# Attention of one encoder layer: TensorE in an order written by hand, long rows beside short ones, output products two steps behind

## The chip, the cores and the metric

The kernel runs on one core of a Trainium2 chip. The metric is device time in microseconds (us) of one execution, the median of several. The engines are TensorE (PE; its weight loads are listed as PEld), VectorE (DVE), ScalarE (ACT), GpSimd (POOL) and SyncE (SP), which issues most DMAs. Each takes its own instructions in order and waits on semaphores for the others.

## The reference, cut to what matters

One layer on a sequence of 2048 positions of width 1024: a norm, one projection to queries, keys and values, two kinds of attention side by side, an output projection, and a gated feed-forward network with a short convolution.

```python
h = rmsnorm(x, attn_norm_g)
qa, ka, va, qb, kb, vb = split(h @ w_in, 6)          # 6 x 512 columns
# A: 8 heads of 64; a query sees 8 chunks of 64 to its left and its own chunk
pa = softmax(qa ka^T / 8 + rel_bias, over the band);  oa = pa @ va
# B: 4 heads of two maps of 64; a query sees all chunks up to its own
p1, p2 = softmax(q1 k1^T / 8 + t5_bias), softmax(q2 k2^T / 8 + t5_bias)
ob = rmsnorm((p1 - lam * p2) @ vb) * subln_g * 0.8
x = x + concat(oa, ob) @ w_out
u = causal_dwconv(rmsnorm(x) @ w_up);  gate, val = split(u)
out = rmsnorm(x + (silu(gate) * val) @ w_down)
```

## The kernel before, in words

Every float32 operand is held as two float16 parts (high and low), and a product is three matmuls (high x high, high x low, low x high).

**Stages.** First the norm of x is transposed into `hT`, four tiles of 512 positions (`make_h`). Then comes attention, in eight passes that are called heads here: `ORDER` is 4, 5, 0, 6, 1, 7, 2, 3, where 4 to 7 are the B heads and 0 to 3 are pairs of A heads. Then comes the output projection (`out_proj`, in two halves of four units), and from there the feed-forward network, which the change does not touch.

**A head** has 16 rows of 128 queries. A row i of a B head reaches over (i+1) x 128 keys; a row of an A head reaches over at most 640. For a row (`attn_a` L452, `attn_b` L503):

1. TensorE computes scores in pieces of up to 512 keys, for two maps, into a bank of PSUM each (`scores`, L426 and L428; four banks in all). The low part of the queries has 64 rows of weights, the high part 128.
2. VectorE adds the bias and takes the running maximum (L474 in A, L524 in B: one instruction for a piece and a map), then the negative scaled maximum (`nb`, L478, L527).
3. ScalarE takes the exponentials with their sums (L481, L530). In B, VectorE forms sums, reciprocal and `ratio` (L533, L536, L538) and subtracts the second map from the first (L546; for some groups ScalarE and GpSimd do it, L543 and L544).
4. ScalarE copies to float16 (`phl`, high part, L482, L548), and the low part is a subtraction: on VectorE for one map of an A row and on GpSimd for the other (L483), on GpSimd in B (L549).
5. SyncE's DMA transposes `phl` into `pt` (in groups of at most 1024 keys), TensorE multiplies `pt` by the values (L495, L557: the output products), and VectorE scales the result into `osb` (L497, L559).

Of the tiles between these steps there are two `phl`, three `pt`, and eight of `St`, the rows of scores.

**Projections.** Beside the rows of a head, TensorE projects the rest of this head's queries and the next head's keys and values, 24 matmuls of 512 columns for 512 positions (`project`, L372). The next head's weights are loaded, scaled and split at the head's start; a small matmul sums their squares over the partitions (L146).

**What sets the order.** A scheduler places each engine's instructions by priority: the order of the program's text, with 1000 places of advantage for the attention rows (`attend`, `HA`) and for the splits of a projection (`HP`). It also weighs when it thinks operands will be ready, so on each engine the rows, the projections and the output products of several rows are mixed.

Of the kernel before, what the change touches and what calls it, by code (L numbers as in the profile page):

```python
# [18 lines left out]
P = 128  # L19
# [13 lines left out]
HA = 1000  # L33
KF = True
# [31 lines left out]
def kernel(  # L66
# [135 lines left out]
    with ExitStack() as at:  # L202
# [116 lines left out]
        def load_w(w, p, j, first=False, raw=None):  # L319
# [3 lines left out]
                             .rearrange("p (c n) -> p c n", c=NC))  # L323
            E, RE, gs = scale_of(all_rows(ss, bank_a), ga, 2.0 ** 13, 2.0 ** -80)
# [40 lines left out]
        def project(w, tg, j):  # L365

            hl, h = w["hl"][j], hT[tg]
            ps = ps_mm.tile([P, TG], F32, name="mm")
            n = 0
            for c in range(NC):  # L370
                for a, b in TERMS:
                    nc.tensor.matmul(ps, lhsT=hl[:, a, c, :], rhs=h[:, b, c, :], start=n == 0, stop=n == 3 * NC - 1)  # L372
                    n += 1
            return ps

        def proj_k(w, tg):

            ks = kv.tile([P, 2, TG], F16, name="ks")
            ps = project(w, tg, 1)
# [3 lines left out]
            return ks  # L383

        def proj_v(w, tg):


            vs = kv.tile([P, 2, 4, P], F16, name="vs")
            if "first" in w:
                hl, h = w["hl"][2], hT[tg]  # L390
                ps = ps_mm.tile([P, 4, P], F32, name="mm")
                for t in range(4):
                    n = 0
                    for c in range(NC):
                        for a, b in TERMS:
                            nc.tensor.matmul(ps[:, t], lhsT=h[:, a, c, t * P:(t + 1) * P], rhs=hl[:, b, c, :],
                                             start=n == 0, stop=n == 3 * NC - 1)
                            n += 1
                with tc.high_priority(offset=HP):
                    split(vs[:, 0], vs[:, 1], ps, QS)  # L400
                return vs
            vt = granule("vt", TG, F16)
            ps = project(w, tg, 2)
# [3 lines left out]
            return vs  # L407

        def proj_q(w, tg):

            qs = kv.tile([P, 2, 2, TG], F16, name="qs", bufs=2)
            ps = project(w, tg, 0)
# [5 lines left out]
            return qs  # L418

        def scores(ps, qs, t, groups, k0, k1):  # L420
# [3 lines left out]
            ks, kc, qc = groups[g][0], slice(k0 - g * TG, k1 - g * TG), slice(t * P, (t + 1) * P)  # L424
# [27 lines left out]
        def attn_a(p, w, qs, groups, tg):  # L452
            osb = sb.tile([P, 4, P], F32, name="osb", bufs=2)
            for t in range(4):
                i = tg * 4 + t
                W = min(i * P, 512) + P
                k0 = (i + 1) * P - W
                N = min(W, 256)
                F = W - N
                mx = tiny.tile([P, 2, 2], F32, name="mx")  # L460
                l = tiny.tile([P, 2], F32, name="l")
                nb = tiny.tile([P, 2], F32, name="nb")
                hl = sb.tile([P, 2, 2, W], F16, name="phl", tag="HL", bufs=2)
                pt = sb.tile([P, 2, 2, W // P, P], F16, name="pt", tag="PT", bufs=3)
                Sm, m = [granule("St", W) for hd in range(2)], [BIG, BIG]
                for part, (a, b) in enumerate(((F, W), (0, F))):
                    if a == b:
                        continue
                    ps = [ps_s.tile([P, 512], F32, name="s") for hd in range(2)]
                    for ka, kb in pieces(k0 + a, k0 + b, ()):  # L470
                        scores([p_[:, ka - k0 - a:kb - k0 - a] for p_ in ps], qs, t, groups, ka, kb)
                    for hd in range(2):
                        bias = w["far"][:, hd, 384 - F:] if part else w["near"][:, hd, 256 - N:]
                        V.tensor_tensor_reduce(Sm[hd][:, a:b], ps[hd][:, :b - a], bias, 1.0, m[hd],  # L474
                                               ALU.add, ALU.max, mx[:, hd, part:part + 1])
                        m[hd] = mx[:, hd, part:part + 1]

                V.tensor_scalar(nb, mx[:, :, 1 if F else 0], w["nsc"], LN14, ALU.mult, ALU.add)  # L478
                for hd in range(2):
                    St = Sm[hd]  # L480
                    A.activation(St, St, AF.Exp, bias=nb[:, hd:hd + 1], scale=w["sc"], accum_out=l[:, hd:hd + 1])  # L481
                    A.activation(hl[:, 0, hd], St, AF.Copy)  # L482
                    (nc.gpsimd if hd in AP else V).tensor_tensor(hl[:, 1, hd], St, hl[:, 0, hd], ALU.subtract)  # L483
                nc.sync.dma_start_transpose(pt.rearrange("p a h b q -> p (a h b) q"),
# [239 lines left out]
        for _ in out_proj(1):  # L724
            pass
# [531 lines left out]
```

## Time and profile before

| what | value |
|---|---|
| median of 3 runs | 2564.09 us (2552.84 to 2574.48) |
| profiled execution | 2562.97 us, its span 2560.9 us |
| busy in the span | PE 2389.8, DVE 1894.7, ACT 1401.5, POOL 1171.0 us |
| mean granted TensorE clock | 0.956 |
| attention and output projection | to 1315.6 us, where the first matmul of the feed-forward network starts |

A head's stretch is read from VectorE's first instruction of a row: the heads start near 95, 265, 433, 526, 698, 791, 962 and 1059 us, and the last row's output products end near 1218 us. [...]

### The profile page before, as it was taken

Reading aid. Unit: us, or ns where it says so; the run is one execution under the profiler, and the core shown is the slowest. Engines: PE = TensorE matmul, PEld = TensorE weight load, DVE = VectorE, ACT = ScalarE, POOL = GpSimd, SP = SyncE. Lnnn points to the kernel's source line nnn. Section 1 sums busy time; section 2 is a strip of 40 time slices with the busy share of each in tenths; the row PEclk is TensorE's granted clock in tenths of the full one; section 3 lists DMA queues with packets and bytes.
Section 4 is the critical chain, followed back from the end, with each engine's and each line's share of the span. In section 5 each row is a group of like instructions: output and inputs, shape, how many; then the busy total and the mean of one; then the engine's idle time right before and its main releaser. Section 6 shows DMA issues by size and latency. Waiting matters only on the chain.

```text
span 2560.9 us, 39466 instructions
## 1 busy us (share of the span) xinstructions
PE 2389.8 (93%) x13878; PEld 1146.9 (45%) x13878; DVE 1894.7 (74%) x4391; ACT 1401.5 (55%) x2431; POOL 1171.0 (46%) x1127
## 2 busy tenths in 40 slices
PE   5799998989897999989869999999999999999998
PEld 4544444544454444444434444444444444444443
DVE  6669786877876797757665888888887886656545
ACT  5547556755675567655434656665656564323322
POOL 2315334332433252123343566656665664756654
PEclk8898998989898989989989999999999999999999
DMA  7224545863677359989978333333323329323322
GB/s 211 57 54 88 104 78 103 143 128 73 112 134 137 58 105 200 191 177 255 278 203 207 123 110 116 100 128 104 122 95 126 104 92 404 121 89 110 112 87 78
DMA packets 631222, 340.48 MB, mean 133 GB/s; under 512 B 448920, under 2 KB 597712, under 8 KB 629616
## 3 DMA queue, kind: packets, MB, share of 16 engines
q1 hardware_dynamic: 615264, 316.15, 48.7%
q10 hardware_dynamic: 12592, 10.26, 1.5%
q0 software_dynamic: 3168, 11.56, 1.4%
q8 instruction: 108, 1.77, 0.3%
q14 instruction: 90, 0.74, 0.1%
HBM read 148.87 MB, written 85.21 MB: 91 GB/s over the span
## 4 chain that ended last, share of the span: by engine, by line
PE 53%; DMA 8%; DVE 8%; issue 4%; ACT 4%; POOL 2%; SPq 2%; ACTq 0%; DVEq 0%; POOLq 0%
PE mm L762 27%; PE mm L1161 13%; PE mm L372 7%; DMA pt<-phl 5%; PE omm L625 2%; PE s L428 2%; DMA wd<-gd 2%; PE s L426 1%; SPq L996 1%; PE o L557 1%; DVE St L524 1%; ACT St L481 1%; ACT phl L482 1%; DVE hl L649 1%; DVE St L546 1%
## 5 line engine op out<-in xcount | busy, mean ns | idle before, releaser
L762 PE MATMUL mm<-T,wuhl 128*128 128x512 f16 x3696 | 802.8, 380 | 24.8 <-ACT tmp L933 22.4
L762 PEld LDWEIGHTS <-wuhl 128*128 128x128 f16 x3696 | 361.9, 98 | 457.8 <-issue 25.9
L372 PE MATMUL mm<-h,whl 128*128 128x512 f16 x2208 | 535.1, 389 | 0.1
L1161 PE MATMUL mm<-wd,ghl 128*128 128x512 f16 x1848 | 401.8, 380 | 2.9 <-ACT ghl L127 1.8
L372 PEld LDWEIGHTS <-whl 128*128 128x128 f16 x2208 | 205.7, 100 | 250.1 <-issue 38.2
L549 POOL TENSOR_TENSOR phl<-St,phl 128x1024 f16<-128x1024 f32 (+4 forms) x96 | 155.7, 1632 | 304.2 <-ACT phl L548 292.6
L1161 PEld LDWEIGHTS <-ghl 128*128 128x128 f16 x1848 | 180.7, 98 | 223.4 <-ACT ghl L127 2.9
L961 DVE SCALAR_TENSOR_TENSOR Y<-U,taps,Y 128x1024 f32<-128x1024 f32 x176 | 257.3, 1462 | 3.9 <-ACT Y L957 2.4
L530 ACT ACTIVATE St<-St,nb,sc 128x1024 f32<-128x1024 f32 (+4 forms) x192 | 188.1, 981 | 88.3 <-DVE nb L527 87.5
L426 PE MATMUL s<-ks,qs 128*128 128x128 f16 (+3 forms) x720 | 196.1, 303 | 41.7 <-DVE mxb L524 32.7
L127 ACT ACTIVATE ghl<-wd,gsc 128x384 f16<-128x384 f32 (+1 forms) x176 | 106.6, 659 | 195.6 <-DMA wd<-gd 89.7
L128 DVE SCALAR_TENSOR_TENSOR ghl<-wd,gsc,ghl 128x384 f16<-128x384 f32 (+1 forms) x176 | 136.9, 812 | 95.1 <-ACT ghl L127 94.4
L524 DVE CUSTOM_DVE_ANT_0 St<-s,near,mxb 128x512 f32<-128x512 f32 (+3 forms) x280 | 168.7, 624 | 40.6 <-PE s L428 34.7
L483 POOL TENSOR_TENSOR phl<-St,phl 128x640 f16<-128x640 f32 (+2 forms) x64 | 82.4, 1287 | 243.8 <-ACT phl L482 198.7
L428 PE MATMUL s<-ks,qs 64*128 64x128 f16 (+3 forms) x720 | 182.8, 307 | 0.0
L625 PE MATMUL omm<-wohl,oT 128*128 128x512 f16 x672 | 159.2, 391 | 8.7 <-DVE x L629 8.6
L871 POOL TENSOR_TENSOR Sx<-wuraw 128x512 f32<-128x512 f32 x44 | 77.8, 1769 | 171.5 <-ACT wuraw L862 153.9
L965 ACT ACTIVATE Y<-Y 128x1024 f32<-128x1024 f32 x44 | 46.5, 1057 | 179.7 <-DVE Y L961 179.7
L557 PE MATMUL o<-vs,pt 128*128 128x128 f16 x1632 | 123.9, 231 | 21.0 <-DMA pt<-phl 16.4
L792 DVE SCALAR_TENSOR_TENSOR wdhl<-wdraw,wd_sc,wdhl 128x128 f16<-128x128 f32 x132 | 134.6, 1038 | 11.6 <-ACT wdhl L789 10.9
L428 PEld LDWEIGHTS <-qs 64*128 64x128 f16 x720 | 54.4, 93 | 180.9 <-issue 165.2
L481 ACT ACTIVATE St<-St,nb,sc 128x640 f32<-128x640 f32 (+4 forms) x128 | 107.9, 844 | 39.8 <-DVE nb L478 36.7
(227 smaller groups left out, 3868.6 us busy)
## 6 DMA issues: line engine op xcount, KB each, us to landing
wd<-gd SPq DMA_DIRECT2D x88, 256.0 KB, 2.8
wuraw<-in_w_up_dram SPq DMA_DIRECT2D x42, 512.0 KB, 5.0
gd<-Y SPq DMA_DIRECT2D x42, 512.0 KB, 5.3
wdraw<-in_w_down_dram SPq DMA_DIRECT2D x154, 128.0 KB, 2.8
wd<-wdd SPq DMA_DIRECT2D x11, 1792.0 KB, 12.0
wdd<-wdhl SPq DMA_DIRECT2D x41, 448.0 KB, 2.6
wraw<-in_w_in_dram SPq DMA_DIRECT2D x24, 512.0 KB, 4.3
td<-hl SPq DMA_DIRECT2D x24, 512.0 KB, 4.0
```

Of the source, the lines that this page charges most:

```text
L128: V.scalar_tensor_tensor(lo, src, scale, hi, ALU.mult, ALU.subtract)
L372: nc.tensor.matmul(ps, lhsT=hl[:, a, c, :], rhs=h[:, b, c, :], start=n == 0, stop=n == 3 * NC - 1)
L426: nc.tensor.matmul(ps[hd], lhsT=qs[:, hd, 0, qc], rhs=ks[:, hd, kc], start=True, stop=False)
L428: nc.tensor.matmul(ps[hd], lhsT=qs[a:b, hd, 1, qc], rhs=ks[a:b, hd, kc], start=False, stop=True)
L524: V.tensor_tensor_reduce(Sm[hd][g][:, a0:a0 + b - a], ps[hd][:, :b - a], bias, 1.0, m[hd], ALU.add, ALU.max, mx[:, hd, f:f + 1])
L530: A.activation(Sm[hd][g], Sm[hd][g], AF.Exp, bias=nb[:, hd:hd + 1], scale=w["sc"], accum_out=l[:, hd, g:g + 1])
L549: nc.gpsimd.tensor_tensor(hl[:, 1], Sm[0][g], hl[:, 0], ALU.subtract)
L557: nc.tensor.matmul(o, lhsT=pt[:, a_, j], rhs=vs[:, c_, kt % 4, :], start=kt == 0 and k_ == 0, stop=kt == i and k_ == 2)
L625: nc.tensor.matmul(ps[n], lhsT=oc[:, a], rhs=wo[ORDER[c]][:, b, n * TG:(n + 1) * TG], start=k == 0, stop=k == 3 * NC - 1)
L762: nc.tensor.matmul(ps, lhsT=hl[:, a, wop, c * P:(c + 1) * P], rhs=Tt[:, b, c, :], start=start and k == 0, stop=k == 11, skip_group_check=n ...
L961: V.scalar_tensor_tensor(Y, self.U[j][:, tap:D + tap], self.u.taps[j][:, tap:tap + 1], Y, ALU.mult, ALU.add)
L1161: nc.tensor.matmul(ps[m].rearrange("p (c n) -> p c n", c=4), lhsT=g[kb][:, a, go], rhs=wd[kb][:, :, c_, wo_], start=kb == k0 and k == 0, s ...
```

## The change

The generators of a head are split, and the order of TensorE is the order of the program's text (`manual_schedule` for PE); the other engines are still placed by the scheduler.

- A row is now a *front* (scores to the transpose) and a *back* (the output products). A step is one front, with a `yield` after each piece of scores. The back of a row runs two steps later (`LAG = 2`), its products behind the first pieces of that step.
- Each step also takes a fixed share of projections: 48 units of six 512-column matmuls (or twelve of 256) for a head's 16 steps, three a step (32 units in the seventh head, 28 over eleven steps in the last).
- Rows of a B head go 0, 15, 1, 14, and so on to 7, 8. Queries are projected in halves of 256 positions, in the order in which the rows need them.
- Weights are fetched and their squares summed (`scan_w`) some steps before they are scaled (`load_w`), at fixed steps (`beside`).
- The last head takes part of its own keys and values, and the first half of the output projection follows in its last five steps and behind it, four or eight units at a time.

```diff
-        def project(w, tg, j):
+        def project(ps, hl, h, t0, t1, step):
...
-                    nc.tensor.matmul(ps, lhsT=hl[:, a, c, :], rhs=h[:, b, c, :], start=n == 0, stop=n == 3 * NC - 1)
+                    nc.tensor.matmul(ps, lhsT=hl[:, a, c, :], rhs=h[:, b, c, t0:t1], start=n == 0, stop=n == 3 * NC - 1)
                     n += 1
-            return ps
+                    if n % step == 0 and n < 3 * NC:
+                        yield
...
+        def proj_q(w, k):
+            i0 = w["halves"][k] * 2
+            ps = ps_mm.tile([P, 2 * P], F32, name="mq", tag="mm")
+            yield from project(ps, w["hl"][0], hT[i0 // 4], i0 % 4 * P, (i0 % 4 + 2) * P, 12)
...
+        def back_a(w, i):
+            pt, rl, k0 = w["P"].pop(i)
...
+        def units(n):
...
+            return q[:2] + k[:2] + q[2:4] + k[2:] + q[4:] + v[:2] + qx + v[2:]
+
+        def beside(n):
...
+            if n + 1 < NH2:
+                x = ws[n + 1]
+                todo[3, 0] = lambda: scan_w(x, ORDER[n + 1], 2)
+                todo[4, 1] = lambda: load_w(x, 2)
...
+        CHUNKS = {NH2 - 2: 32, NH2 - 1: 28}
+        UNTIL = {NH2 - 1: 11}
+
+        def attention():
...
+            for n, w in enumerate(ws):
+                fill, side, got = units(n), beside(n), 0
+                steps = UNTIL.get(n, NT)
+                for s_, i in enumerate(w["order"]):
...
+                    if len(behind) >= LAG:
+                        bw, bi = behind.pop(0)
+                        back = [(back_a if bw["p"] < 4 else back_b)(bw, bi)]
+                    want = CHUNKS.get(n, 48) * (s_ + 1) // steps - got if s_ < steps else 0
+                    got += want
+                    for k in range(slots):
+                        with tc.high_priority(offset=HA):
+                            next(fr)
+                        if (s_, 0) in side and k == 0:
+                            side[s_, 0]()
+                        with tc.high_priority(offset=HA):
+                            pull(back, 2)
+                        pull(fill, want * (k + 1) // slots - want * k // slots)
...
+                    behind.append((w, i))
+                    if n == NH2 - 1 and s_ >= steps:
+                        pull([first], 4)
+                for u in fill:
+                    run(u)
+            while behind:
+                bw, bi = behind.pop(0)
+                with tc.high_priority(offset=HA):
+                    run((back_a if bw["p"] < 4 else back_b)(bw, bi))
+                pull([first], 8)
+            run(first)
+            run(out_proj(1))
+
+        with tc.manual_schedule(engines={mybir.EngineType.PE}):
+            attention()
```

**Where instructions move, first place: VectorE in the middle of an A head.** `phl` is the subtraction of a row (step 4 above), `osb` the scaling of a row's output products, `rl` the reciprocal that it uses (so it names the row), and `St<-s` a row's scores. Before, in the third head (the subtraction is that of row 8, and `rl_5376` belongs to row 5):

```order
L483 TENSOR_TENSOR phl_5647<-St_5650,phl_5647 128x640
L497 TENSOR_TENSOR osb_5276<-o_117,rl_5376 128x128
L487 RECIPROCAL rl_5679<-l_5645 128x2
L474 ISA St_5781,mx_5776<-s_5791,far_3196,mx_5776 128x384
...
L483 TENSOR_TENSOR phl_5715<-St_5718,phl_5715 128x640
...
L497 TENSOR_TENSOR osb_5276<-o_117,rl_5444 128x128
```

Now, in the fifth head (`rl_9056` belongs to the row of `phl_8946`, and `rl_9152` to that of `phl_9061`):

```order
L494 TENSOR_TENSOR phl_8946<-St_8949,phl_8946 128x640
L484 ISA St_9063,mx_9058<-s_9123,far_7700,mx_9058 128x384
...
L498 RECIPROCAL rl_9152<-l_9059 128x2
L519 TENSOR_TENSOR osb_9169<-o_117,rl_9056 128x128
L494 TENSOR_TENSOR phl_9061<-St_9064,phl_9061 128x640
L484 ISA St_9159,mx_9154<-s_9207,far_7700,mx_9154 128x384
...
L519 TENSOR_TENSOR osb_9169<-o_117,rl_9152 128x128
L494 TENSOR_TENSOR phl_9157<-St_9160,phl_9157 128x640
```

Before, a row's subtraction stood ahead of the scaling of the third row back; now it stands behind the scaling of the row just before it.

**Second place: VectorE in a B head.** `lb`, `rl`, `ratio` and `St<-St` are the sums, reciprocal, ratio and subtraction of maps of a row, `nb` is its maximum, and `St<-s` are its scores. Before, near the end of the first head: `lb_2377` to `St_2379` are of row 11, `s_26..` and `nb_2595` of row 12, and `rl_2232` belongs to row 9:

```order
L559 TENSOR_SCALAR osb_2103<-o_117,rl_2232,u_565 128x128
...
L533 TENSOR_TENSOR lb_2377<-lb_2377 128x2
L524 ISA St_2596,mxb_2600<-s_2625,near_562,mxb_2600 128x512
...
L536 RECIPROCAL rl_2422<-lb_2377 128x2
...
L546 SCALAR_TENSOR_TENSOR St_2379<-St_2381,ratio_2424,St_2379 128x1024
...
L524 ISA St_2598,mxb_2600<-s_2634,near_562,mxb_2600 128x512
...
L527 TENSOR_SCALAR nb_2595<-mxb_2600,nsc_558,lnk_93 128x2
```

Now, at the first head's second long row: `lb_1488`, `rl_1573` and `St_1490` are of row 15, and `s_1655` to `s_1756` and `nb_1648` of row 14:

```order
L543 ISA St_1652,mxb_1653<-s_1655,near_562 128x256
...
L553 TENSOR_TENSOR lb_1488<-lb_1488 128x2
L556 RECIPROCAL rl_1573<-lb_1488 128x2
L558 TENSOR_SCALAR ratio_1575<-rl_1573,lb_1488,nlam_92 128x1
L566 SCALAR_TENSOR_TENSOR St_1490<-St_1492,ratio_1575,St_1490 128x1024
...
L543 ISA St_1650,mxb_1653<-s_1693,near_562,mxb_1653 128x128
...
L593 TENSOR_SCALAR osb_1667<-o_117,rl_1573,u_565 128x128
L543 ISA St_1650,mxb_1653<-s_1733,near_562,mxb_1653 128x512
...
L543 ISA St_1651,mxb_1653<-s_1756,near_562,mxb_1653 128x512
...
L547 TENSOR_SCALAR nb_1648<-mxb_1653,nsc_558,lnk_93 128x2
```

Before, row 12's scores ran beside row 11's softmax, and what was scaled was row 9. Now the last three of row 14's five pieces, and its maximum, stand behind the scaling of row 15's finished output products.

## Rows read from the trace of the kernel before

**Rows 1.** Windows: length, busy PE, PEld, DVE, ACT, POOL (instructions); clock, DMA share, GB/s.

```profile
265.00:433.00 168.00, 152.03 (x946) 75.03 (x944) 131.13 (x401) 97.18 (x194) 58.34 (x35) 0.89 0.48 91
433.00:526.00 93.00, 91.66 (x767) 46.96 (x766) 68.57 (x218) 65.77 (x129) 24.27 (x17) 0.98 0.77 135
1218.00:1316.00 98.00, 89.40 (x398) 39.50 (x395) 63.95 (x108) 46.07 (x64) 40.53 (x29) 0.95 0.87 243
```

**Rows 2.** Two windows of 50 us, same columns.

```profile
500.00:550.00 50.00, 38.45 (x412) 22.27 (x412) 41.98 (x129) 33.82 (x69) 19.22 (x13) 0.82 0.90 166
800.00:850.00 50.00, 37.17 (x212) 18.09 (x213) 29.74 (x84) 19.12 (x42) 16.57 (x11) 0.83 0.45 90
```

**Rows 3.** Waits of PE from 95 to 1316 us: total, times, longest.

```profile
PE s L426 <- DVE mxb L524: 32.7, 24, 4.7
PE o L557 <- DMA pt<-phl: 16.4, 5, 8.1
```

**Rows 4.** Timeline of PE in an A head: start, length, instruction, count.

```profile
742.97 3.41 PE L372 MATMUL mm<-h,whl 128*128 128x512 f16 x15
746.22 0.86 PE L495 MATMUL o<-vs,pt 128*128 128x64 f16 x24
746.92 0.49 PE L426 MATMUL s<-ks,qs 128*128 128x384 f16 x2
...
747.61 0.39 PE L426 MATMUL s<-ks,qs 128*128 128x256 f16 x2
...
748.15 1.04 PE L372 MATMUL mm<-h,whl 128*128 128x512 f16 x4
```

**Rows 5.** Timeline of PE in B heads, same columns.

```profile
883.75 1.51 PE L557 MATMUL o<-vs,pt 128*128 128x128 f16 x24
885.10 0.22 PE L426 MATMUL s<-ks,qs 128*128 128x128 f16 x1
...
895.85 0.61 PE L426 MATMUL s<-ks,qs 128*128 128x512 f16 x2
...
896.71 0.60 PE L372 MATMUL mm<-h,whl 128*128 128x512 f16 x2
```

**Rows 6.** Timeline of DVE after the output products of Rows 4.

```profile
747.12 0.29 DVE L497 TENSOR_TENSOR osb<-o,rl 128x128 f32<-128x128 f32 x1 [0.16 <-PE o L495]
```

**Rows 7.** Groups by line and shape, A heads: count, busy us, mean ns, idle.

```profile
L478 DVE TENSOR_SCALAR nb<-mx,nsc 128x2 f32<-128x2 f32 x64 | 17.4, 272 | 0.6
L481 ACT ACTIVATE St<-St,nb,sc 128x640 f32<-128x640 f32 x96 | 87.4, 911 | 37.0 <-DVE nb L478 34.5 <-DVE rl L487 1.8 <-ACT qs L127 0.5
L482 ACT ACTIVATE phl<-St 128x640 f16<-128x640 f32 x96 | 65.7, 725 | 38.7 <-DMA pt<-phl 38.4
L483 DVE TENSOR_TENSOR phl<-St,phl 128x640 f16<-128x640 f32 x48 | 58.3, 1215 | 28.5 <-ACT phl L482 28.4
```

**Rows 8.** The same for the B heads.

```profile
L524 DVE CUSTOM_DVE_ANT_0 St<-s,near,mxb 128x512 f32<-128x512 f32 x168 | 121.7, 746 | 20.1 <-PE s L428 15.5 <-issue 3.0
L527 DVE TENSOR_SCALAR nb<-mxb,nsc,lnk 128x2 f32<-128x2 f32 x64 | 35.1, 549 | 0.5
L530 ACT ACTIVATE St<-St,nb,sc 128x1024 f32<-128x1024 f32 x80 | 98.5, 1231 | 57.0 <-DVE nb L527 56.9
L546 DVE SCALAR_TENSOR_TENSOR St<-St,ratio 128x1024 f32<-128x1024 f32 x36 | 58.1, 1615 | 0.7
L548 ACT ACTIVATE phl<-St 128x1024 f16<-128x1024 f32 x40 | 42.0, 1051 | 36.8 <-issue 13.3 <-DVE St L546 11.3 <-DVE mxb L524 6.0
L549 POOL TENSOR_TENSOR phl<-St,phl 128x1024 f16<-128x1024 f32 x40 | 87.2, 2183 | 118.4 <-ACT phl L548 110.5 <-issue 7.7
```

**Rows 9.** DMA issues, 730 to 800 us (A): count, median us to landing.

```profile
pt<-phl SPq DMA_TRANSPOSE x14, 4.9
```

**Rows 10.** DMA issues, 150 to 250 us (B): count, median us to landing.

```profile
pt<-phl SPq DMA_TRANSPOSE x14, 4.3
```

**Rows 11.** Timeline of PE before the first head's fifth row.

```profile
122.76 0.58 PE L146 MATMUL am<-ws_ss,ones 128*128 128x1 f32 x2 [4.44 <-ACT whl L140]
```

More of the change, by code (lines that the diff above doesn't have):

```diff
@@ L33 @@
 HA = 1000
+NH2 = 8
+LAG = 2
 KF = True
@@ L317, in fetch_w, with scan_w @@
             return raw
-        def load_w(w, p, j, first=False, raw=None):
+        def scan_w(w, p, j, raw=None):
             raw = raw or fetch_w(p, j)
@@ L382, in proj_k @@
                 split(ks[64:128, 1], ks[0:64, 1], ps[64:128], QS)
-            return ks
+            yield
         def proj_v(w, tg):
[L388 to L401, printed above, removed]
+            ps = ps_mm.tile([P, TG], F32, name="mm")
+            yield from project(ps, w["hl"][2], hT[tg], 0, TG, 6)
+            vs = w["v"][tg] = kv.tile([P, 2, 4, P], F16, name="vs")
             vt = granule("vt", TG, F16)
-            ps = project(w, tg, 2)
             with tc.high_priority(offset=HP):
@@ L652, in out_proj, with weights, run @@
                         hl.rearrange("p n a d -> p n (a d)"))
-                yield
-        def weights():
-            return {"hl": {}, "E": {}}
-        w = weights()
-        w["first"] = True
-        groups, qn = {}, None
+        def weights(n):
+            p = ORDER[n]
+            order = list(range(NT)) if p < 4 else [i for a in range(NT // 2) for i in (a, NT - 1 - a)]
+            halves = []
+            for i in order:
+                if i // 2 not in halves:
+                    halves.append(i // 2)
+            return dict(p=p, order=order, halves=halves, hl={}, E={}, raw={}, k={}, v={}, q={}, P={}, o={}, ssq={})
+        def run(unit):
+            for _ in unit:
+                pass
+        w = weights(0)
         xts, raws = [], []
@@ new lines, with pull @@
+        CHUNKS = {NH2 - 2: 32, NH2 - 1: 28}
+        UNTIL = {NH2 - 1: 11}
+        def attention():
+            behind = []
+            def pull(todo, k):
+                for _ in range(k):
+                    while todo:
+                        try:
+                            next(todo[0])
+                            break
+                        except StopIteration:
+                            todo.pop(0)
+            for n, w in enumerate(ws):
+                fill, side, got = units(n), beside(n), 0
+                steps = UNTIL.get(n, NT)
+                for s_, i in enumerate(w["order"]):
+                    a = w["p"] < 4
+                    with tc.high_priority(offset=HA):
+                        fr = (front_a if a else front_b)(w, i)
+                        slots = sum(1 for _ in pieces(0, (i + 1) * P, ((i + 1) * P - min((i + 1) * P, 256),))) if not a \
+                            else (1 if i < 2 else 2)
+                    back = []
+                    if len(behind) >= LAG:
[11 more added lines that the diff above has]
+                        pull(fill, want * (k + 1) // slots - want * k // slots)
+                        if (s_, 1) in side and k == 0:
+                            side[s_, 1]()
+                    with tc.high_priority(offset=HA):
+                        run(fr)
+                        for g in back:
+                            run(g)
+                    behind.append((w, i))
[5 more added lines that the diff above has]
+                bw, bi = behind.pop(0)
+                with tc.high_priority(offset=HA):
+                    run((back_a if bw["p"] < 4 else back_b)(bw, bi))
+                pull([first], 8)
+            run(first)
+            run(out_proj(1))
```

361 lines of the change are left out of this document (190 added, 171 removed).

## The prediction

> **What bounds the kernel now.** I read the windows first, a head at a time. In a B head (265 to 433 us) TensorE is busy 152 of 168 us and VectorE 131; in an A head (433 to 526 us) TensorE is busy 92 of 93 us and VectorE 69 [rows 1]. So TensorE is the bound of attention, with gaps in the B heads only. The waits say what ends the gaps: a bank of scores that VectorE has not read yet (32.7 us in all) and a transpose that has not landed (16.4 us) [rows 3]. Where a quarter of a stretch is idle, the granted clock was 0.82 and 0.83 [rows 2], so a gap also makes the work after it dearer.
>
> What the change can win is therefore the gaps, and a little of TensorE's own work. What it can lose is read from the softmax between a row's scores and its output products, which before had the time of about three rows and now has two steps.
>
> **TensorE's own work.** At the full clock 15 projection matmuls start within 746.22 - 742.97 = 3.25 us, 0.217 us each; 24 output products of an A row take 0.70 us, 0.029 each; four score matmuls of a piece take 0.69 us at 384 keys and 0.54 at 256 [rows 4]. In B 24 output products take 1.35 us, 0.056 each, and a piece of 512 keys 0.86 us [rows 5]; by the two differences a piece of 128 keys takes about 0.38.
>
> - A step of an A head: 18 x 0.217 = 3.9 us of projections, 30 x 0.029 = 0.9 of output products, pieces of 0.54 and 0.69: 6.0 us.
> - Two steps of a B head (a long and a short row, 17 key tiles together): 36 x 0.217 = 7.8, 51 x 0.056 = 2.9, and about 6.4 pieces of 4.1 us in all: 14.8 us, so 118 us a head.
>
> Queries in halves make twice as many matmuls of half the columns. A 128-column product already starts every 0.056 us [rows 5], so I cost a 256-column one at half of 0.217: nothing added. Their splits and copies double in number on VectorE and ScalarE; VectorE has 37 us to spare in a B head [rows 1], which covers them. Without that cover they would add at most as much again as now, some 1.4 us for each half, and 16 x 1.4 = 22 us a head. Weights that are fetched and summed a step earlier take away waits like the 4.4 us of [rows 11]; if the sums were late again it would be that, once a head. All of this is small beside the next two points.
>
> **An A head: a ring through VectorE.** In VectorE's new order a row's subtraction stands behind the scaling of the row before it, and that waits for output products, which wait for the transpose of that row, which waits for its subtraction. VectorE takes its instructions in order, so the rows can't overlap there: subtraction 1.2 us [rows 7], issue to landing 4.9 [rows 9], output products 0.9 and about 0.16 until the last is written (0.86 against 0.70) [rows 4], scaling 0.29, and three handovers of 0.04 (747.08 to 747.12) [rows 4, 6]: 7.6 us for a row, where TensorE has work for 6.0. The same comes from the other side: from the last scores to the landing are two reads of about 0.6 us, `nb` 0.27, two exponentials 0.91, two copies 0.73, the subtraction and the transpose, 11 us in all [rows 7, 9], and TensorE's order holds 2.6 + 6.0 + 0.54 = 9.1 us between them. With some queueing on the DMAs I take 7.7. Twelve rows have five key tiles, four are shorter and run at TensorE's 6.0: 12 x 7.7 + 4 x 6.0 = **116 us**, against 93 now.
>
> **A B head: a ring through the long rows.** The last three pieces of row 14 stand behind row 15's output products on TensorE, and row 14's softmax can't start before its last piece. The ring for row 14, from the landing of row 15:
>
> - output products 24 + 24 and a piece of 128 keys between: 1.35 + 0.38 + 1.35; then 6 projections, two pieces of 512, 6 projections, a last piece: 1.3 + 1.7 + 1.3 + 0.86; together 8.2 us [rows 4, 5]; the last two reads of VectorE 2 x 0.75 [rows 8]: 9.7.
> - `nb` 0.55, four exponentials of 1.23 (two of them 1/8 narrower) 4.6, three small VectorE steps at 0.27 0.8, subtraction of the maps 1.6, copy 1.05, low part 2.2 [rows 7, 8], transpose 4.3 [rows 10], and seven handovers 0.3: 15.4.
>
> That is 25.1 us for two rows. Between the last score and the first output product TensorE has only 6.4 us of other work (24 projections, two small pieces, three output products), so the cover falls short by 9. Row 8, the narrowest, comes out the same way at 7.7 + 13.6 = 21.3. The seven rings from row 14 to row 8 average 23.3 us, 163 in all, and row 15 behind the head before it takes 25: **188 us** a head, against 168 to 172 now.
>
> **The sum.** Before the first long row TensorE needs the same keys and values as before, and the first weight sums, until about 123 us [rows 11]. Then 4 x 188 + 4 x 116 = 1216. Behind the last landing there are 8 + 28 + 64 units of the output projection: the second half takes 98 us as now [rows 1], the other 36 units 36 x 6 x 0.217 = 47, the last products 1: 146. So the feed-forward network starts at 123 + 1216 + 146 = 1485 us instead of 1315.6, which is +169, at the full clock. The clock comes on top: at 0.83 [rows 2] TensorE's share of the rings (8.2 us in 32 of them, 1.0 in 48) would be a fifth dearer, 32 x 1.6 + 48 x 0.2 = 61 us; since a slower TensorE also has fewer gaps, I take half, 30. The profiled execution of 2563 us lies 1 us under the median, so no correction is made: 2563 + 169 + 30 = **2762 us**. The upper bound of the forecast's own range is the whole clock price and 0.9 us more for each transpose in B, as long as in A: 2563 + 169 + 61 + 32 x 0.6 to 0.9, about 2820, and some 50 more where the weights' work on GpSimd and ScalarE falls into the rings; the lower is both rings at 10% less: 2640.
>
> **The rivals.**
>
> - *The waits are covered* (the other side). Then a B head goes at VectorE's 131 us and an A head at TensorE's 96: 123 + 4 x 131 + 4 x 96 + 146 = 1177, and 2563 - 139 = 2424 us. It decides at a chain under 6.4 us in B and 9.1 in A. For it speaks that pieces of both maps issued together save TensorE 0.4 us each; against it the sums above, from durations that were measured.
> - *Only the A ring binds, and B gains a little over now*: B at 150 to 160 us gives 1333 to 1373, 2580 to 2620 us; at 140, 2540. This is the case of no change.
> - *TensorE falls to the lower clock.* By rows, 0.82 and 0.83 came with a quarter idle [rows 2], and in the rings 20 to 37% of TensorE's time is a wait that comes once a row. [...] Against it: a TensorE that is slower than the ring has no gaps, and its clock came back wherever it was busy (0.98 from 433 to 526 us [rows 1]). [...]
>
> That the order isn't as the text says can be left out: the rows of VectorE's order stand in the program.
>
> **How the numbers follow.** The rings 0.78, waits covered 0.10, only A 0.06, lower clock 0.06. Runs of this kernel tell about 1% (26 us) from no change. Faster by over 1% are the covered case and a trace of the third: 0.11; within 1%: 0.05; slower: 0.84. The range takes in the rings with both bounds and part of the third and fourth case: 2615 to 2900; what it leaves out is the covered case, most of the case of no change, and the clock's far end.
>
> **What would show it.** Right: TensorE's waits led by the transpose, before the output products of both kinds, some 30 to 80 us for the A heads and 200 to 280 for the B heads; A rows 7 to 8.5 us apart, long B rows 21 to 26; VectorE less busy in attention than the 131 of 168 us now. Wrong: TensorE over 95% busy in attention, or transposes landing before TensorE asks for them.

## The result, and the profile after

The changed kernel takes 2943.81 us (median of 4 runs, 2937.77 to 2950.55), the kernel before 2564.77 in the same session: a ratio of 1.148, 95% interval 1.142 to 1.154. The forecast was 2762 us, 2615 to 2900. The side and the mechanism were as forecast, the size was not: 379 us instead of 198. The profiled run took 2948.0 us, with a span of 2946.2.

Windows of the changed kernel, the columns of [rows 1]: a B head, an A head, the feed-forward network.

```profile
315.00:537.00 222.00, 133.01 (x1006) 82.92 (x1007) 130.21 (x406) 96.81 (x199) 60.31 (x34) 0.80 0.32 66
537.00:674.00 137.00, 109.10 (x957) 65.29 (x954) 80.69 (x270) 72.86 (x150) 33.49 (x23) 0.89 0.55 109
1674.00:2946.00 1272.00, 1214.17 (x5588) 549.15 (x5588) 907.45 (x1442) 633.88 (x984) 741.11 (x855) 0.98 0.40 128
```

The B head takes 222 us instead of 168, and no engine has more to do: VectorE's 130.2 us are as before, TensorE's 133.0 are 19 fewer. The A head takes 137 instead of 93. In the B head all that is added is idle time: TensorE is idle for 89 us instead of 16. In the A head it is idle for 28 us instead of 1, and its busy time grows by 17 us, with 957 matmuls instead of 767 and the granted clock at 0.89 instead of 0.98. TensorE's waits from 95 to 1545 us say for what, as against [rows 3]:

```profile
PE o L589 <- DMA pt<-phl: 353.4, 32, 13.7
PE o L515 <- DMA pt<-phl: 108.5, 40, 7.4
```

32 waits are one for each long row of the four B heads. One of them is read best with the work between two of them, TensorE's timeline from row 15 to row 14 of the second head (start, length, instruction, count, idle before it):

```profile
360.49 2.74 PE L589 MATMUL o<-vs,pt 128*128 128x128 f16 x24 [13.73 <-DMA pt<-phl]
363.02 0.42 PE L438 MATMUL s<-ks,qs 128*128 128x128 f16 x2
...
363.60 1.51 PE L589 MATMUL o<-vs,pt 128*128 128x128 f16 x24
364.95 1.46 PE L376 MATMUL mm<-h,whl 128*128 128x512 f16 x6
366.24 0.59 PE L438 MATMUL s<-ks,qs 128*128 128x512 f16 x2
...
370.11 1.47 PE L376 MATMUL mm<-h,whl 128*128 128x512 f16 x6
371.41 0.38 PE L438 MATMUL s<-ks,qs 128*128 128x256 f16 x2
...
374.11 2.79 PE L376 MATMUL mq<-h,whl 128*128 128x256 f16 x24
376.74 0.38 PE L438 MATMUL s<-ks,qs 128*128 128x256 f16 x2
377.05 0.28 PE L440 MATMUL s<-ks,qs 64*128 64x256 f16 x2
390.44 2.74 PE L589 MATMUL o<-vs,pt 128*128 128x128 f16 x24 [13.10 <-DMA pt<-phl]
```

The pieces of row 14 stand behind the products of row 15, as forecast; row 14's last scores are read at 371.6; TensorE runs out of other work at 377.3; the transpose lands at 390.4. Landing to landing is 30.0 us, where the forecast's ring had 25.1.

In the table a head begins with VectorE's first read of its scores, and the last A head ends with its last output product; both are read from the timelines.

| kernel | us | B heads, us | A heads, us |
|---|---|---|---|
| before | 2565 | 170, 167, 172, 172 | 93, 93, 96, 159 |
| changed | 2944 | 221, 222, 218, 215 | 137, 137, 143, 157 |
| e1, LAG 3 | 2599 | 163, 163, 159, 150 | 107, 110, 114, 145 |
| e2, products last in the step | 2602 | 164, 156, 156, 162 | 108, 104, 115, 137 |
| e3, natural order in B | 2807 | 186, 187, 178, 176 | 140, 141, 151, 156 |
| e4, scheduler's order | 2535 | 163, 152, 149, 144 | 105, 105, 94, 125 |
| e7, e1 and e2 together | 2550 | 152, 151, 146, 150 | 104, 105, 103, 146 |
| e8, A subtraction on GpSimd | 2967 | 221, 222, 219, 217 | 143, 141, 156, 153 |
| e13, TensorE kept busy in B | 2915 | 212, 212, 209, 206 | 138, 133, 144, 162 |
| e11, scheduler's order, LAG 3 | 2502 | 151, 151, 136, 134 | 110, 107, 91, 130 |

### The profile page after: what moved, and what is told of

It is laid out like the page before. It is cut to its first block, busy times and chain, and to the rows that moved or that the text cites. A ratio compares the mean times of both kernels' runs of the same rounds, so it can differ in the third digit from the quotient of the medians.

```text
span 2946.2 us, 41300 instructions
## 1 busy us (share of the span) xinstructions
PE 2371.9 (81%) x14646; PEld 1246.4 (42%) x14646; DVE 1886.2 (64%) x4455; ACT 1411.6 (48%) x2495; POOL 1164.2 (40%) x1127
## 5 line engine op out<-in xcount | busy, mean ns | idle before, releaser
L589 PE MATMUL o<-vs,pt 128*128 128x128 f16 x1632 | 148.6, 265 | 353.4 <-DMA pt<-phl 353.4
L376 PEld LDWEIGHTS <-whl 128*128 128x128 f16 x2976 | 288.6, 103 | 191.8 <-issue 35.2
L376 PE MATMUL mm<-h,whl 128*128 128x512 f16 x1440 | 357.3, 392 | 3.7 <-ACT whl L338 2.1
L543 DVE CUSTOM_DVE_ANT_0 St<-s,near,mxb 128x512 f32<-128x512 f32 (+2 forms) x280 | 164.8, 625 | 231.6 <-PE s L440 211.9
L589 PEld LDWEIGHTS <-pt 128*128 128x128 f16 x1632 | 129.4, 122 | 368.0 <-DMA pt<-phl 359.0
L569 POOL TENSOR_TENSOR phl<-St,phl 128x1024 f16<-128x1024 f32 (+7 forms) x96 | 162.1, 1699 | 247.6 <-ACT phl L568 243.3
L376 PE MATMUL mq<-h,whl 128*128 128x256 f16 x1536 | 211.3, 298 | 0.0
L515 PE MATMUL o<-vs,pt 128*128 128x64 f16 x1680 | 69.3, 204 | 119.0 <-DMA pt<-phl 108.5
L438 PE MATMUL s<-ks,qs 128*128 128x128 f16 (+3 forms) x720 | 161.0, 308 | 0.0
L896 DVE SCALAR_TENSOR_TENSOR wdhl<-wdraw,wd_sc,wdhl 128x128 f16<-128x128 f32 x132 | 136.0, 1047 | 18.2 <-ACT wdhl L893 17.5
L568 ACT ACTIVATE phl<-St 128x1024 f16<-128x1024 f32 (+7 forms) x96 | 75.9, 802 | 144.5 <-DMA pt<-phl 116.3
```

Of the source, the lines that this page charges most:

```text
L376: nc.tensor.matmul(ps, lhsT=hl[:, a, c, :], rhs=h[:, b, c, t0:t1], start=n == 0, stop=n == 3 * NC - 1)
L438: nc.tensor.matmul(ps[hd], lhsT=qs[:, hd, 0, qc], rhs=ks[:, hd, kc], start=True, stop=False)
L543: V.tensor_tensor_reduce(Sm[hd][g][:, a0:a0 + b - a], ps[hd][:, :b - a], bias, 1.0, m[hd], ALU.add, ALU.max, mx[:, hd, f:f + 1])
L569: nc.gpsimd.tensor_tensor(hl[:, 1], Sm[0][g], hl[:, 0], ALU.subtract)
L589: nc.tensor.matmul(o, lhsT=pt[:, a_, j], rhs=vs[:, c_, kt % 4, :], start=kt == 0 and k_ == 0, stop=kt == i and k_ == 2)
L896: V.scalar_tensor_tensor(dst, src, scale, h, ALU.mult, ALU.subtract)
```

## The experiments

### Is it the distance?

e1 takes the distance from two steps to three, e2 leaves two and issues a row's output products behind the step's last piece of scores, e7 does both. Nothing is removed and no buffer added.

```diff
-LAG = 2
+LAG = 3                       # e1, e7
-                            pull(back, 2)
+                            pull(back, 0)       # e2, e7
```

> Only the number LAG is changed, from 2 to 3: output products stand three steps behind, all buffers stay. Theory (two steps are too short for the softmax; rings through TensorE's order): the third step puts another 6 us of TensorE's work before the output products of an A row and some 8.5 us before those of a long B row. A heads come to about 100 us instead of 137, B heads to 140 to 160 instead of 219; attention near 1270 us, the kernel 2500 to 2580 us, and TensorE's waits for the transpose fall from 462 us to under 120. Rival (the order by steps, the pairing of long with short rows or the lower clock cost the time, not the distance): the heads stay within 10% of 137 and 219, the kernel above 2850 us. Second rival: three transpose buffers hold no third step in B, since a long row takes two of them: A falls to about 100, B stays near 219, about 2790 us.

> The distance stays 2, but within a step the output products are issued behind the step's last scores and projections instead of from its first piece on. Theory: the pieces of a long row no longer stand behind the output products of the long row before it, and nearly a whole step is added between a row's last scores and its products (B: about 17 us of TensorE's work against a softmax of 18.8; A: about 12 against 11 to 13). B heads 130 to 160 us, A heads 100 to 110, the kernel 2480 to 2600 us. Rival (the distance in steps is what counts, not the place within the step): B stays near 219 and A near 137, above 2850 us.

> TensorE in program order, three steps of distance and the output products behind the step's last piece; x1k as in the change. Theory: the two lengthenings of the cover add, so the waits for the transpose in B (54 and 68 us with one of them) fall under 20 us; B heads 135 to 150 us, bounded by VectorE's 131, A heads 97 to 104; the kernel 2510 to 2560 us. Rival (what is left with either one is not the distance but the three transpose buffers and the one bank of output products): B stays at 150 to 163, the kernel 2580 to 2610 us.

e1 took 2599 us (ratio 1.013, 1.009 to 1.016), e2 2602 (1.014, 1.010 to 1.018), e7 2550 (0.994, 0.993 to 0.997). Each alone gives back 342 to 345 of the 379 us, with all of the change's other parts in place: the distance is the cause. The rivals (the order by steps, the pairs of long and short rows, the lower clock by itself) are out, and so is the second rival of e1, the three transpose buffers, which are as before; e2 also shows that what counts is TensorE's work between scores and products, not the number of steps. e1 is 19 us above its range and e2 2 us, and e7 shows what took the wait's place, in TensorE's waits from 95 to 1300 us:

```profile
PE s L438 <- DVE mxb L543: 59.0, 65, 3.5
...
PE o L589 <- ACT o L594: 20.1, 9, 11.0
PE o L589 <- DMA pt<-phl: 14.4, 8, 3.9
```

The transpose is down from 353.4 us to 14.4. What is late next is a bank of scores that VectorE has not read, and the one bank of output products, which ScalarE's square still holds. Of the 151 us of the second B head TensorE works 124 and VectorE 131.

### Does the pairing of long and short rows cost by itself?

```diff
-order = list(range(NT)) if p < 4 else [i for a in range(NT // 2) for i in (a, NT - 1 - a)]
+order = list(range(NT))
```

> B heads take their rows in natural order, 0 to 15, instead of long beside short; LAG stays 2. Theory: two rows are then in flight in every ring, so a ring (11 us of TensorE and VectorE and 18.8 of softmax for the longest row, about 3 and 6 for the shortest) covers two rows of like length: the sum over 16 rows is 165 to 185 us a B head instead of 219; A heads stay at 137; the kernel 2750 to 2830 us. Rival (the order of the rows does not matter, since lag alone does): B heads within 10 us of 219, about 2940 us.

2807 us (1.094, 1.090 to 1.098), B heads 176 to 187 (165 to 185 were expected): as the theory says. With a distance of two, natural order has two long rows in flight, the pairing only one, so in the change each long row's ring is paid in full; TensorE's waits for the transpose in B are 202.8 us here instead of 353.4. The pairing costs 137 us with TensorE in program order at a distance of two. Where the scheduler orders TensorE it costs nothing at the same distance (e12, below); in program order with three steps no run tells.

### Which ring holds the A rows?

VectorE in the changed kernel, two A rows of the fifth head (columns as in the timeline above):

```profile
953.83 0.29 DVE L519 TENSOR_TENSOR osb<-o,rl 128x128 f32<-128x128 f32 x1 [1.03 <-PE o L515]
954.03 0.96 DVE L494 TENSOR_TENSOR phl<-St,phl 128x640 f16<-128x640 f32 x1
...
962.68 0.29 DVE L519 TENSOR_TENSOR osb<-o,rl 128x128 f32<-128x128 f32 x1
...
963.78 0.83 DVE L494 TENSOR_TENSOR phl<-St,phl 128x640 f16<-128x640 f32 x1 [0.25 <-ACT phl L493]
```

The first subtraction starts right behind the scaling of the row before it, as the forecast's ring says. The second waits for ScalarE's copy: its row is held by its scores, which stand on TensorE behind the products of two rows back. e8 takes the first ring away (`AP = (0,)` to `AP = (0, 1)`).

> The changed kernel, but both subtractions of an A row are on GpSimd (AP = (0, 1)); VectorE then has none that stands behind the scaling of the row before. If the prediction's ring through VectorE is what sets the 8.7 us of an A row, A rows come to 6.0 to 7 us, A heads to 105 to 115 instead of 137 to 143, the kernel 2830 to 2870 us. If the ring through TensorE (scores of a row behind the output products two rows back, 17.2 us for two rows) binds as tightly, taking away the first leaves the second: A heads 130 to 145 us, the kernel 2920 to 2965 us.

2967 us (1.157, 1.152 to 1.162), A heads 141 to 156, above its range. The ring through VectorE is not what holds the rows alone: without it they come no closer together. That the ring through TensorE is just as long by itself is not shown, since e8 lengthens that ring too: both subtractions of 1.4 us now follow each other on GpSimd.

### What is the lower clock worth?

Windows of the changed kernel around the gap shown above: the products behind it, the work that follows, and last the gap itself.

```profile
360.40:367.00 6.60, 6.51 (x62) 4.93 (x62) 1.04 (x5) 0.82 (x3) 0.67 (x1) 0.76 0.42 78
367.00:377.00 10.00, 10.00 (x76) 6.14 (x74) 8.10 (x32) 5.36 (x10) 1.05 (x1) 1.00 0.01 2
347.00:360.40 13.40, 0.00 (x0) 0.00 (x0) 5.26 (x14) 6.82 (x14) 6.76 (x3) 0.61 0.43 89
```

In the 6.6 us behind an idle stretch of 13.4 us the granted clock is 0.76 of full speed as a mean. In windows of 2 us it is 1.00 from 340 to 348 us, 0.97 in the next, 0.50 from 350 to 362, 0.62 from 362 to 364, and 1.00 from there to 380. The first 24 products, at 360.49, take 2.74 us, and the next 24, from 363.60, take 1.51 again. e9 and e13 put matmuls that nothing uses into the gaps before the long rows' products, e9 36 for every row, e13 a number for each row.

```diff
+    if k == 0 and back and bw["p"] >= 4 and bi >= 8:
+        warm = ps_mm.tile([P, TG], F32, name="warm", tag="mm")
+        for _ in range(FILL[bi]):        # e9: 36
+            nc.tensor.matmul(warm, lhsT=bw["v"][0][:, 0, 0, :], rhs=bw["k"][0][:, 0, :], start=True, stop=True)
     pull(back, 2)
```

> The changed kernel with 36 extra matmuls of 512 columns before the output products of each long B row (32 rows); their results are used by nothing. They fall into the gaps of 8 to 13.7 us in which TensorE waits for the transpose (36 x 0.217 = 7.8 us), so TensorE is busy until shortly before the output products. Theory: the lower clock behind each gap costs 24 output products 2.53 us instead of 1.35 and a little more behind them, on the ring; with the gap filled each ring is 1.2 to 1.4 us shorter, 32 rings: the kernel 38 to 45 us faster, 2898 to 2912 us, B heads about 209. Rival (the clock is no part of the ring, or the fill delays the products as much as it saves): 2935 to 2960 us.

> As the kernel with 36 extra matmuls before the output products of each long B row, but with a number for each row (56, 48, 50, 51, 47, 38, 36, 41 for rows 15 to 8), worked out from the gaps that the changed kernel showed, so that TensorE is busy until less than 1 us before the transpose lands. Theory: what decides the clock is the idle time just before the output products; with it gone, every ring gains what row 9 gained with a remaining gap of 1 us, 2.3 us (24 output products in 1.35 instead of 2.53 us, twice in the longest rows): 32 x 1.6 to 2.3 = 51 to 74 us against 2944, so 2870 to 2893 us; of the 4.1 us by which a ring was forecast too short, about half is then the clock and half the work inside the softmax. Rival (row 9 gained by something else, the clock is worth the 18 us of the first fill): 2915 to 2935 us.

e9 took 2926 us (1.142, 1.138 to 1.145), e13 2915 (1.136, 1.132 to 1.141): 18 and 29 us less than the change, in e13's B heads 9 to 10 us each. e9 falls between theory and rival, e13 on the lower end of its rival's range. Products of e9 behind four gaps of different length that were left:

```profile
356.80 2.74 PE L589 MATMUL o<-vs,pt 128*128 128x128 f16 x24 [5.97 <-DMA pt<-phl]
...
388.04 1.51 PE L589 MATMUL o<-vs,pt 128*128 128x128 f16 x24 [3.09 <-DMA pt<-phl]
...
472.28 2.74 PE L589 MATMUL o<-vs,pt 128*128 128x128 f16 x24 [2.86 <-DMA pt<-phl]
...
520.94 1.51 PE L589 MATMUL o<-vs,pt 128*128 128x128 f16 x24 [0.16 <-DMA pt<-phl]
```

The idle time just before the products does not decide alone, as e13's theory has it: they are fast behind 3.09 us and slow behind 2.86. The part of the ring from the products to the last read of the next row's scores came down, as a mean over rows 14 to 8 of four heads, from 10.30 us to 9.91 (e9) and 8.96 (e13). A B head of e13, with the granted clock at 0.99:

```profile
315.00:525.00 210.00, 198.97 (x1360) 106.24 (x1359) 127.96 (x397) 95.08 (x195) 59.82 (x34) 0.99 0.37 70
```

So the clock is worth 1.34 us a ring, and some 40 us for 32 of them (an estimate). The four B heads of e13 together come to 839 us instead of 876, its A heads to 578 instead of 574; what made the A heads longer is not shown.

### The feed-forward network

Its 27 us were no part of the forecast. The change also has an edit that its list leaves out: `x1k`, a tile for rows of x in the output projection, lay in the pool of the queries (tag `qs`) before and lies in the pool of the attention rows (tag `HL`) now. The network's first weights, on SyncE's queue of the changed kernel, are fetched only after the output projection, which ends at 1674, behind two transposes of its result:

```profile
1668.60 12.52 SPq L1100 DMA_TRANSPOSE T<-td  x2
1681.17 1.21 SPq L942 DMA_DIRECT2D wuraw<-in_w_up_dram  x2
```

Before, the same fetch was issued at 1224 us, 92 us ahead of the network. e5 moves x1k out of the pool of the attention rows.

```diff
-xt = sb.tile([P, D], F32, name="x1k", tag="HL", bufs=2) if pc and sd else \
+xt = wpool.tile([P, D], F32, name="x1k", tag="whl", bufs=4) if pc and sd else \
```

> The changed kernel with one line put otherwise: the tile x1k of the output projection lies in the pool of the weights (the tag whl) instead of the pool of the attention rows (the tag HL). In the changed kernel the feed-forward network takes 1272 us from the end of the output projection, 27 more than before, its first weights are fetched at 1681 us instead of some 92 us ahead of its start, and TensorE waits 22.7 us for them. Theory: those weights lie where x1k lies, so they wait for the last x1k. Then they are fetched again during the output projection, the network takes about 1245 us, and the kernel comes to about 2917 us (2905 to 2930). Rival (the steps by themselves push the weights back): no change, 2935 to 2955 us.

2937 us (1.145, 1.140 to 1.150). Windows of e5, the output projection behind the last head and the network:

```profile
1545.00:1695.00 150.00, 134.56 (x599) 59.66 (x598) 90.61 (x152) 62.53 (x84) 50.42 (x37) 0.93 0.79 230
1695.00:2937.00 1242.00, 1209.46 (x5591) 547.96 (x5588) 912.81 (x1424) 618.79 (x961) 725.32 (x842) 0.99 0.40 129
```

The network is back at 1242 us, so the place of x1k is what held its weights. But the output projection takes 150 us instead of 130, and TensorE waits 15.4 us there for VectorE, which it did not in the changed kernel; that the weights' work beside it is the reason is argued. The theory was right for the network and wrong for the sum: the time lies in the rival's range, and the 7 us that are left are within the two intervals (1.140 to 1.150 and 1.142 to 1.154). As far as these runs tell, the wait was moved and not saved.

### TensorE's order by the scheduler, and what beats both

```diff
-with tc.manual_schedule(engines={mybir.EngineType.PE}):
-    attention()
+attention()
```

> All of the change stays but TensorE's order, which the scheduler sets again from its estimates, as in the kernel before. Theory: the scheduler puts output products where it estimates their transposes to have landed, so the waits for the transpose go and the heads come back towards 170 and 95 us; 2540 to 2680 us. Rival (steps, halves of queries and pairs of long and short rows cost the time by themselves): above 2800 us.

2535 us (0.988, 0.984 to 0.991), 5 under its range: some 1.2% faster than before, with every other part of the change kept. TensorE's waits for the transpose come to 9.0 us from 95 to 1600 us, though LAG is 2 here too. TensorE's work is dearer than in program order (busy 1100 us from 95 us to the end of the output projection, in e1 1047), because the two maps' pieces run side by side less often (the 168 matmuls of 64 rows and 512 keys are busy 58.9 us against 33.2; in the kernel before, two that stand together, at 896.38 us, take 0.39 us, as long as the one that stands alone at 885.74), and that costs less than the waits. Four runs build on this kernel:

> The change without TensorE's order (the scheduler sets it) and with x1k in the pool of the weights. Theory: the two gains add: 2535 - 27 = 2508 us (2495 to 2520). Rival (the output projection is the bound there and the network's weights only move the wait): 2525 to 2545 us.

> TensorE's order set by the scheduler, x1k in the pool of the weights, and LAG = 3. Theory: where the scheduler sets the order, the distance in steps decides little, since it issues output products where it estimates their transposes landed: 2515 to 2540 us, as with LAG = 2 (2528). Rival (with LAG = 2 the scheduler too is held back by the rings): 2490 to 2510 us.

> TensorE's order set by the scheduler, x1k in the pool of the weights, B rows in natural order. With TensorE in program order natural order was worth 137 us (2944 to 2807), since two long rows were in flight. Theory: under the scheduler that cause is absent; what remains is that long rows at the end of a head ask more of VectorE than a step gives (VectorE 131 us a head, most of it in the last rows): the same or somewhat slower, 2520 to 2570 us. Rival (long beside short costs there too): 2480 to 2510 us.

> TensorE's order set by the scheduler, x1k in the pool of the weights, LAG = 4 (with 2 it took 2528 us, with 3 2502 us). Theory: the scheduler only moves work that the program issues near each other, so the distance in steps still helps it, but with three steps the waits for the transpose are down to 6 us and nothing is left to win: 2490 to 2515 us. Rival (the third step helped through the order of VectorE and the banks of scores, and a fourth does again): 2470 to 2488 us. Second rival (three transpose buffers and one bank of output products hold up the earlier rows): above 2520 us.

e6 took 2528 us (0.985, 0.981 to 0.988), above its range by 8 and in its rival's: as in e5 the network is back at 1241 us and the output projection has grown, from 132 us in e4 to 154, and the 8 us that are left are within the intervals. e11, with LAG 3, took 2502 us (0.976, 0.974 to 0.978), the fastest of all; e14, with LAG 4, 2505 (0.976, 0.973 to 0.980). The theory that the distance decides little under the scheduler fell: the third step is worth 26 us, a fourth nothing. The 26 us lie in the B heads, together 606 us in e6 and 572 in e11 (A heads 429 and 438). From 95 us to the end of the output projection TensorE is busy 1108 us in e6 and 1093 in e11, at a granted clock of 0.96 and 0.97, and idle 81 and 69; how the third step does it stays open. e12 took 2524 us (0.985, 0.983 to 0.988): natural order neither costs nor gains there, at a distance of two.

> TensorE in program order, three steps, output products last in the step, and x1k in the pool of the weights (the kernel with the first three took 2550 us). Theory: x1k there gains what it gained in the changed kernel and in the one ordered by the scheduler, 7 of 2944 and 8 of 2535: 2536 to 2546 us, which is faster than before by about 1% and not better than the scheduler's order (2528). Rival (the network's 27 us come back whole, since attention is shorter here): 2515 to 2530 us.

2555 us (0.996, 0.995 to 0.997), 9 above its range and no better than e7. Here too the network is shorter (1243 us instead of 1272) and the output projection longer (152 instead of 119): the place of x1k gains nothing clear of the noise in e5, e6 or e10.

## Why the prediction was wrong

**Right.** TensorE's waits are led by the transpose, though they are longer than forecast (353.4 and 108.5 us; 200 to 280 and 30 to 80), and in a B head no engine has more work. The ring through the long rows is there piece by piece. e1 and e2 confirm the cause. Queries in halves added nothing that can be seen on TensorE: 24 products of 256 columns follow each other within 376.74 - 374.11 = 2.63 us, 0.110 each, half of 0.217.

**The sum, term by term** (measured from the profile after; the clock is in the terms):

| term | forecast | measured |
|---|---|---|
| until the first scores, and four B heads | 123 + 4 x 188 = 875 | 94 + 876 = 970 |
| four A heads | 4 x 116 = 464 | 574 |
| last products to the end of the output projection | 146 | 130 |
| network | 1245 | 1272 |
| clock on top | 30 | in the terms |

**The step that failed is the length of the B ring.** 25.1 us for row 14 and 23.3 as a mean of seven were sums of the chain's own instructions; measured are 30.0 and 27.4; the long rows come 24.7 to 30.9 us apart, where 21 to 26 was the sign of being right. Row 14's chain from its last read of scores to the landing, all engines of the changed kernel:

```profile
371.68 0.29 DVE L547 TENSOR_SCALAR nb<-mxb,nsc,lnk 128x2 f32<-128x2 f32 x1
372.11 1.23 ACT L550 ACTIVATE St<-St,nb,sc 128x1024 f32<-128x1024 f32 x1
...
375.67 1.12 ACT L550 ACTIVATE St<-St,nb,sc 128x896 f32<-128x896 f32 x1
375.95 1.90 POOL L337 TENSOR_TENSOR wraw<-wraw,ws_gs 128x1024 f32<-128x1024 f32 x1 [14.24 <-DVE ws_gs L158]
...
376.92 0.94 DVE L553 TENSOR_TENSOR lb<-lb 128x2 f32<-128x2 f32 x1 [1.05 <-ACT St L550]
377.79 0.41 DVE L543 CUSTOM_DVE_ANT_0 St<-s,near 128x256 f32<-128x256 f32 x1
...
378.64 0.69 DVE L130 SCALAR_TENSOR_TENSOR ks<-mm,ks 64x512 f16<-64x512 f32 x1
379.37 0.27 DVE L558 TENSOR_SCALAR ratio<-rl,lb,nlam 128x1 f32<-128x1 f32 x1
379.68 4.21 DVE L566 SCALAR_TENSOR_TENSOR St<-St,ratio 128x1024 f32<-128x1024 f32 x2
380.69 2.25 POOL L339 TENSOR_TENSOR whl<-wraw,whl 128x1024 f16<-128x1024 f32 x1 [2.85 <-ACT whl L338]
381.00 1.06 ACT L568 ACTIVATE phl<-St 128x1024 f16<-128x1024 f32 x1 [0.38 <-DVE St L566]
382.91 5.12 POOL L569 TENSOR_TENSOR phl<-St,phl 128x1024 f16<-128x1024 f32 x2
...
385.90 4.03 SPq L571 DMA_TRANSPOSE pt<-phl  x2
```

The exponentials take the 4.6 us of the forecast, the transpose 4.5 instead of 4.3. But the forecast gave three small steps 0.8 us, and from the last exponential (376.8) to the end of `ratio` (379.6) it is 2.8: the addition `lb` alone lasts 0.94 (more on this below), and two reads of the short row beside it and the low part of a key projection stand in between on VectorE. The low part on GpSimd is ready to start when the copy ends at 382.06 and starts at 382.91, behind the weights' `whl`, and then takes until 385.9: 3.8 us instead of 2.2. As a mean of the seven rows the softmax part is 17.1 us instead of 14.6, and the part on TensorE 10.3 instead of 8.7. Of these 4.1 us the clock is 1.3 (e13). For row 14 the trace shows the rest as work of others inside the chain; no run removed that work, so its price is read and not tested. For 32 rings the 4.1 us make 131 us, about the 124 by which the four heads are longer than forecast; the stretch before them was put 29 us too long. The forecast's clock term of 30 us stands against some 40 in the B heads alone.

**The A heads** failed by their size too: rows 6 to 15 of the first two come 8.7 to 8.9 us apart instead of 7.7. From the end of the subtraction to the landing it is 5.5 to 5.7 us, where 4.9 was taken. The ring through VectorE, named as the one that binds, is not alone (e8). The longer rows are some 12 of the 21 us of such a head. The other 9 are its first four rows, which were let run at 6.0: the products of rows 0 and 1 stand behind those of the B head's last long row (in the fifth head row 2's first scores are read at 916 us, 24 us after row 0's). The last two A heads, 143 and 157 us, have the output projection's weights and units among their steps, and in the last one the same stretch to the landing takes 7.3 us; no run separates these. With 110 us in all the A heads miss nearly as much as the B heads.

**The range** ended at 2900 on allowances for the whole price of the clock, longer transposes in B and some 50 us of the weights' work in the rings. The B ring alone was 18% longer than the sum of its own instructions (27.4 to 23.3), and the A heads had no allowance beyond the clock.

**The rivals.** Waits covered and only the A ring binds are out. The lower clock was there: in each of the 32 long rows the first 24 products behind the wait take 2.74 us, where the next 24 in the second head's row 15 take 1.51. But it is not what sets the time: with the clock at 0.99 in the B head shown, e13 gets back 29 us of the 379 (the A heads' clock, 0.92 in the first of them, e13 leaves low). Only the work at the start of a ring runs at the lower clock (0.76 in the 6.6 us behind the gap shown, 1.00 in the 10 us after them), and the rest of the ring is not TensorE's. No run shows TensorE at the lower clock throughout, the far end that the range left out: as means the changed kernel's windows show 0.80 in a B head and 0.89 in an A head.

## What to carry to other kernels

A fixed distance between a producer and its consumer on an engine in program order is worth what that engine does in between, not its number of steps: add up the chain, count the rows in flight, and compare before fixing it; one step more, or the consumer at the end of its step, took no buffer here and gave 342 to 345 us. A chain of measured durations is a lower bound: add what else its engines do in that time (2.5 us on 14.6 here) and the clock behind each gap (1.3 us). A tile moved to another pool can hold back whatever is laid in that pool next; moving it away again can shift the wait instead of saving it.

## What the runs showed of the hardware

Two kinds of VectorE's instructions, both with their operands in SBUF, were longer in the changed kernel where GpSimd worked on tensors at the same time: the addition `lb` 942 ns instead of 157, the subtraction of the maps over 896 keys 3.01 us instead of 1.15. The line of the first (ns shortest/median/longest):

```profile
L553 DVE TENSOR_TENSOR lb<-lb x32: 146/159/943, 127.4 to 1249.3; 128x2 f32<-128x2 f32 x32
```

An addition of two columns takes 157 ns as a mean of the 24 that have no GpSimd tensor instruction beside them, and 942 ns as a mean of the 4 that start in the middle of one, as the one at 376.92 beside L337: it ends at 377.86, and L337 at 375.95 + 1.90 = 377.85. (The other four start less than 0.1 us before such an instruction ends, and take 147 ns.) The reads of scores of 512 keys, which take one operand from PSUM, are not longer beside one: 741 ns as a mean of 11, 747 of the 157 with none beside them. All 4 long additions end less than 0.02 us behind the GpSimd instruction beside them; what makes them wait is not shown.

The same is in row 14's chain in both directions:

```profile
380.69 2.25 POOL L339 TENSOR_TENSOR whl<-wraw,whl 128x1024 f16<-128x1024 f32 x1 [2.85 <-ACT whl L338]
380.88 3.01 DVE L566 SCALAR_TENSOR_TENSOR St<-St,ratio 128x896 f32<-128x896 f32 x1
...
382.91 2.97 POOL L569 TENSOR_TENSOR phl<-St,phl 128x1024 f16<-128x1024 f32 x1
```

The second subtraction of the maps starts beside the weights' L339 and takes 3.01 us; the four of its shape with no GpSimd tensor instruction beside them take 1.15. It is still running when the low part starts on GpSimd, which then takes 2.97 us, where the 24 of its shape with no such VectorE instruction beside them take 2.12. So of the 1.6 us by which the low part was put too short, about half is the wait behind L339 and half this lengthening.
